# Pool weights in a buffer of their own, decay matrices from float32r products, and the last output part's products cut in two

## The chip, the cores and the metric

One core of one Trainium2 chip runs the whole program. The metric is the device time of one execution in microseconds, and a kernel's time is the median over its runs. The engines are PE (TensorE: matmul, with PEld for its weight loads), DVE (VectorE), ACT (ScalarE), POOL (GpSimd) and SP (SyncE), which here issues nearly all DMAs.

## The reference, cut to what matters

One layer of a streaming encoder runs for 1024 prompt tokens and 8 x 16 sample tokens, 1152 columns in all, D = 1024:

```
x = x + 1/2 * SwiGLU_1(RMSNorm(x))
p = RMSNorm(x) @ W_in           # q, k, v, gate: 4 heads x 128; a, b per head; u: 4 pool groups x 128
  A: gated delta rule per head  # gc = cumsum(g); decay_ij = exp(gc_i - gc_j); chunks solved, then state passed on
     o = RMSNorm(o) * SiLU(gate)
  B: d = mean of the last 2/4/8/16 tokens - token;  z = (d @ w_pool[group]) * scale
x = x + concat(o, z) @ W_out
x = x + 1/2 * SwiGLU_2(RMSNorm(x));  y = RMSNorm(x)
```

The change is in the middle part, the mixer. It touches the decay matrix, the pool group's map `d @ w_pool`, and the product with `W_out`.

## The kernel before, in words

The columns are cut into three chunks: chunk 0 has 512, chunks 1 and 2 have 320 each. The program runs the first half step, then the mixer, then the second half step. Most products are float32r in three terms (`mm3`: hi·hi, hi·lo, lo·hi); the operands are split into hi and lo by an ACT cast and a DVE subtraction. Products inside the delta rule are plain float32; each of them stands in the trace as two MATMULs.

**The mixer's order.** The mixer runs in two blocks: A is chunk 0, B is chunks 1 and 2. Its work is cut into tasks with names such as Bm3: block, kind, index. The kinds that matter here are p, v, g (projections), m (projection of a pool group and its means), n (`mapped`: the means times `w_pool`), x (hi/lo split of the mapped means), w and t (`prework` of a head, prompt and sample), y and z (inverses), c and s (the chain of states), and o (split of the gated head output, then `out_part`: 96 matmuls of 320 columns in block B). A loop written out by hand (`rule`, `fill`, `urgent`) picks the next piece of a task by a clock `T.t`, which adds a price for each product (columns / 2400 + 0.003 us for float32r, max(columns, weight columns) / 600 us for float32) and a latency that each `yield` names. A task in `fill` runs when no `urgent` one is due. A scheduler below that settles the order on each engine, so one changed price can move many instructions.

**What the change touches**, by the names and lines of this kernel:

- `means` (L1379): at its end, L1412 and L1413, it takes the small slot `wpl` in region A6 and asks for the group's 128 x 128 pool weights. `wpl` is one slot. It also holds the sample history `so` of block B (L1392), which is copied out by a DMA to `spool` (L1394), so the pool weights can't land before that DMA has read it.
- `mapped` (L1416): per chunk one float32 product `wpl` x `z` into a ps_d bank, then an ACT scale.
- `prework` (L1098): L1119 makes the decay differences, one 128 x 128 float32 product for each 128 tokens: the column of `gfl` spread over 128 as weights, a triangular matrix as the moving operand. There are 16 of them in block A and 20 in block B, 36 in all.
- `out_part` (L1071) and `oz_split` (L1084): task o splits the gated output of its head (`ozh`, `ozl`, 640 columns at once), then multiplies it and the mapped means (`om`) with the same output weights, for 2 halves of the weights, 2 chunks and 4 row tiles. The head's products and the means' products of one row tile stand together in one ps_d bank.
- Task x of index 3 waits for task o of index 2, since both use the one `omh`, `oml` pair in region B3.

The PSUM tags a, b, c and d have two banks each; the chain uses c, the inverses and prework b, the projections a, the output products and `mapped` d. The second half step opens with products for chunk 0 (`ps_b<-A,O`, `ps_a<-A,O`, 512 columns), which don't need the mixer's last results.

Of the kernel before, what the change touches and what calls it, by code (L numbers as in the profile page):

```python
# [40 lines left out]
def trunk(ctx: ExitStack, tc: tile.TileContext, xin, s0, convst, poolst, cm_in, vec_in, small_in,  # L41
# [54 lines left out]
    def region(tag, dt=F32):  # L96
        return main.tile([P, SIZE[tag]], dt, tag=tag, name=nm(tag))
# [92 lines left out]
    def load_mix(src, kind):  # L190
        with tc.high_priority(offset=300):
            return load_unit(src)
# [713 lines left out]
    def cmat(c):  # L906
        return cm[:, c:c + P]

    ms.place(region("A5"), ("Xs", 768, 1), ("DT", 512, 1), ("MV", 512, 1), ("DTs", P, 1), ("Vns", P, 1))
    ms.place(region("A6"), ("z", WIDE, 1), ("Vc", 64, 1), ("Uc", 64, 1), ("tu", 64, 1), ("wpl", P, 1), ("sso", 4, 3), ("tt", 4, 3),  # L910
             ("half", 8, 1), ("small", 8, 1), ("nega", NH, 1), ("cout", 36, 1), ("Xss", 192, 1), ("Vc", 64, 1), ("vn", P, 2),
             ("sc", 120, 2), ("av", 80, 1), ("gm", 32, 1))
    ms.place(region("R2"), ("eglS", 32, 1), ("osbs", P, 1), ("scout", 288, 1), ("Vcs", 16, 2), ("Ucs", 16, 1), ("tus", 16, 1), ("sqr", 320, 1))
    ms.place(region("B0"), ("k", 640, 1), ("q", 640, 1), ("gate", 640, 2))
    ms.place(region("B6"), ("k", 640, 1), ("q", 640, 1), ("kd", 512, 2), ("r", P, 1), ("rs", P, 1))
    ms.place(region("B1"), ("Vn", 512, 2), ("Tt", 512, 1), ("merge", 512, 1), ("U", 512, 1))
# [35 lines left out]
    def mix_block(blk, hb, extra, zrow):  # L952
# [16 lines left out]
        def decays():  # L969

            ab = mt("raw", 640)[:16]
            for (o, n), (hi, lo) in zip(offs, H):
                pa = pt("a")[:16, :n]
                for k in range(KT):
                    T.matmul(pa, wab[:, k, :], hi[k], start=(k == 0), stop=False)
                    T.matmul(pa, wab[:, k, :], lo[k], start=False, stop=(k == KT - 1))
                V.tensor_mul(ab[:, o:o + n], pa, RS[:16, o:o + n])
            pab = pt("b")[:, :nu * 16].rearrange("p (u c) -> p u c", c=16)
            for u in range(nu):
                T.transpose(pab[:, u, :], ab[:, u * P:(u + 1) * P], ident[:16, :16])  # L980
            av = mt("av", 5, 16)[:, :nu]
            V.tensor_copy(av, pab)
            def col(i, w=4):
                return sc[:, i, :nu * 4].rearrange("p (u h) -> p u h", h=4)

            def bc(t):
                return t.unsqueeze(1).to_broadcast([P, nu, NH])

            a_, b_ = col(0), col(1)
            V.tensor_add(a_, av[:, :, 0:4], av[:, :, 8:12])  # L990
            V.tensor_add(b_, av[:, :, 4:8], av[:, :, 12:16])
            V.tensor_tensor(a_, a_, bc(small[:, 0:NH]), ALU.add)
            e_ = col(2)
            V.scalar_tensor_tensor(e_, a_, -1.0, a_, ALU.mult, ALU.min)
            A.activation(e_, e_, AF.Exp)
            A.activation(e_, e_, AF.Ln, bias=1.0)
            V.scalar_tensor_tensor(a_, a_, 0.0, e_, ALU.max, ALU.add)
            V.tensor_tensor(a_, a_, bc(nega), ALU.mult)
            A.activation(b_, b_, AF.Exp, scale=-1.0)
            V.tensor_scalar(b_, b_, 1.0, None, ALU.add)  # L1000
            V.reciprocal(b_, b_)
            yield 7
            pc = pt("b")
            T.matmul(pc[:, 0:16], cmat(C_TRI), gfl[:, 0:16], start=True, stop=True)
            T.matmul(pc[:, 20:36], cmat(C_STRIL), gfl[:, 0:16], start=True, stop=True)
            T.matmul(pc[:, 40:56], ones, gfl[:, 0:16], start=True, stop=True)
            if nu == 5:
                T.matmul(pc[:, 16:20], cmat(C_TRIS), gfl[:, 16:20], start=True, stop=True)
                T.matmul(pc[:, 36:40], cmat(C_STRILS), gfl[:, 16:20], start=True, stop=True)
                gm = mt("gm", NB, NH)  # L1010
                V.tensor_tensor(gm, cm[:, C_IND:C_IND + 8].unsqueeze(2).to_broadcast([P, NB, NH]),
                                gfl[:, 16:20].unsqueeze(1).to_broadcast([P, NB, NH]), ALU.mult)
                T.matmul(pc[:, 64:96], ones, gm.rearrange("p b h -> p (b h)"), start=True, stop=True)
            V.tensor_copy(gc, pc[:, 0:nu * 4])
            A.activation(negegc, gc, AF.Exp)
            V.tensor_scalar(negegc, negegc, -1.0, None, ALU.mult)
            A.activation(ekd, pc[:, 20:20 + nu * 4], AF.Exp)
            A.activation(egl[:, :16], pc[:, 40:56], AF.Exp)
            if nu == 5:
                A.activation(eglS.rearrange("p b h -> p (b h)"), pc[:, 64:96], AF.Exp)  # L1020
            yield 4
# [46 lines left out]
            A.activation(y[:, :nt], y[:, :nt], AF.Silu)  # L1068
            return y

        def out_part(h, *parts):  # L1071
            for j in range(2):
                w = load_mix(wout[2 * h + j], 'o')
                for (o, n), c in zip(offs, chunks):
                    for d in range(4):
                        po = pt("d")[:, :n]
                        for i, (hi, lo) in enumerate(parts):
                            mm3(po, w[0][:, 4 * i + d, :], w[1][:, 4 * i + d, :], hi[:, o:o + n], lo[:, o:o + n], i == 0, i == 1)
                        x = xk(c, 4 * j + d)
                        with tc.high_priority(offset=0):  # L1080
                            V.tensor_add(x, x, po)  # L1081
                        yield 0

        def oz_split(src, hi=None, lo=None, e=None):  # L1084
            if hi is None:
                hi, lo = mt("ozh", 640), mt("ozl", 640)
            A.copy(hi[:, :nt], src)  # L1087
            (e or V).tensor_sub(lo[:, :nt], src, hi[:, :nt].bitcast(F32))
            return hi, lo

        def p3(n):
# [6 lines left out]
        def prework(h, q, k, v, samp):  # L1098

            c0, n, u0 = (512, 1, 4) if samp else (0, 4, 0)  # L1100
            tri = cmat(C_TRIS if samp else C_TRI)
            low = cmat(C_LOWS if samp else C_LOW)
            kc = [k[:, c0 + u * P:c0 + (u + 1) * P] for u in range(n)]
            qc = [q[:, c0 + u * P:c0 + (u + 1) * P] for u in range(n)]
# [11 lines left out]
            pg = p3(n)  # L1116
            for u in range(n):
                i = (u0 + u) * 4 + h
                T.matmul(pg[:, u], gfl[:, i:i + 1].to_broadcast([P, P]), tri, start=True, stop=True)  # L1119
            DT = get("DT", n, P)  # L1120
            for u in range(n):
                i = (u0 + u) * 4 + h
# [255 lines left out]

        def means(g):  # L1379
            win_ = WINS[g]  # L1380
            w = load_mix(win[16 + g], 'm')
            raw = mt("raw", WIDE)
            sv = raw[:, 527:527 + NB * 31].rearrange("p (b t) -> p b t", b=NB)
# [15 lines left out]
            for src, base, dst, L in parts:  # L1399
# [9 lines left out]
                    rec = cm[:, C_REC + g * 16:C_REC + g * 16 + 16]  # L1409
                    V.tensor_tensor(sm[:, 0, 0:16], sm[:, 0, 0:16], rec, ALU.mult)  # L1410
                V.scalar_tensor_tensor(dst, sm, 1.0 / win_, src[:, :, HIST:], ALU.mult, ALU.subtract)
            wpl = mt("wpl", P)  # L1412
            SY.dma_start(wpl, wpool_in[g])  # L1413
            return z, wpl

        def mapped(g, z, wpl):  # L1416
# [2 lines left out]
                T.matmul(ps, wpl, z[:, o:o + n], start=True, stop=True)  # L1419
                A.mul(z[:, o:o + n], ps, vec[:, 80 + g:81 + g])  # L1420

        kq, gt, pv, pw, pws, mz, om = {}, {}, {}, {}, {}, {}, {}

        def part_of(w, h):

# [31 lines left out]
                mapped(NH - 1 - h, *mz[h])  # L1457
                yield 0.8
            if w == "x":
                om[h] = oz_split(mz[h][0][:, :nt], mt("omh", 640), mt("oml", 640))  # L1460
                yield 1.5
            if w == "o":
                oz = oz_split(gt[h][:, :nt])
                yield 1.5
                yield from out_part(h, oz, om[h])
                return 0.5
            if w == "r":
                for c in (1, 2):
                    for _ in rstd_parts(c, pair(z2, mt("sqr", 320)), R[c], step=1):
                        yield 2  # L1470
# [47 lines left out]
            return spill()  # L1518
        return blocks[b](w, int(name[2]))

    names = [b + w + str(h) for b in "AB" for w in "pvgmowycnx" for h in range(NH)] + ["Ad0", "Bd0", "Ar0", "BH0", "BX0"]
    names += ["B" + w + str(h) for w in "tzs" for h in range(NH)]
    after = {n: set() for n in names}

# [6 lines left out]
        return n[:2] + str(i) if i >= 0 else "A" + n[1] + str(i + NH) if n[0] == "B" and "A" + n[1] + "0" in after else None  # L1531

    for n in names:
        if n[1] in "dHXr":
            continue
        b, w, h = n[0], n[1], n[2]
        need = {"w": "pvd", "y": "w", "t": "pvd", "z": "t", "c": "yg", "s": "zg", "n": "m", "x": "n", "o": "cx"}.get(w, "")
        rule(n, *[b + i + ("0" if i == "d" else h) for i in need])
        behind = {"v": "wt", "c": "c", "m": "n" if b == "A" else "nx", "x": "xo"}.get(w, w)
        for i in behind:  # L1540
            rule(n, prev(b + i + h))
        if w in "wt":
            rule(n, prev(b + ("c" if w == "w" else "s") + h, 2))
        if w == "m" and b == "A":
            rule(n, prev("Ax" + h, 2))
        if w == "o" and b == "B":
            rule(n, "Bs" + h)
        if w in "pgvmd" and b == "B":
            rule(n, "BH0")
        if b == "B" and w in "ts" or n in ("Bp2", "Bg2"):  # L1550
            rule(n, "BX0")
    rule("Ap3", "Ac0")
    rule("Ag3", "Ao0")
    rule("Bp0", "Ac1")
# [10 lines left out]
    for n in after:  # L1565
        after[n] &= set(names)

    fill = "Av0 Ap0 Av1 Ag0 Am0 Ap1 Ap2 Ag1 Av2 Ag2 Ao0 Am1 Ap3 Av3 Am2 Am3 Ao1 Ag3 Ao2 Bp0 Bg0 Bv0 Ao3 Bp1 Bv1 Bm0 Bg1 Bp2 Bv2 Bm1 Bp3 Bo0 Bg2 Bv3 Bo1 Bm2 Bg3 Bm3 Bo2 Bo3".split()
    urgent = [n for n in names if n not in fill]
    rank = {w: i for i, w in enumerate("drHXcsywtxnz")}  # L1570
    urgent.sort(key=lambda n: (n[0], rank[n[1]], n[2]))
# [221 lines left out]
```

## Time and profile before

| what | us |
|---|---|
| median of 3 runs (2152.22 to 2154.87) | 2153.16 |
| the profiled execution's own time | 2155.54 |
| its span | 2153.7 |
| PE busy in it | 2102.3 |
| the mixer's stretch, roughly | 740 to 1358 of the span |

Times inside the profile are microseconds from the start of the span. A busy PE is a PE with a matmul in flight; the start of a matmul is given, its end is modelled, so the time of one in a dense run is read from start to start. An entry in square brackets behind a timeline row is the idle time of the engine before it and who ended it.

### The profile page before, as it was taken

To read this page: it belongs to the slowest core of one execution; us is meant where nothing else is said; L and a number is where in the kernel's file an instruction comes from. 1 tells how busy PE (TensorE), PEld (TensorE's weight loads), DVE (VectorE), ACT (ScalarE), POOL (GpSimd) and SP (SyncE) were. 2 spreads that over 40 slices of the span, in tenths; PEclk is the share of its full clock that TensorE was granted. 3 is DMA by queue.
4 is the path that set the end of the run, shared out by engine and by line. 5 is a ranking of instruction groups with operands and counts; after the bars stand their busy time and mean duration, and the time that the engine had idled before them with its cause. 6 is when DMAs were issued, how large, how long until landed. Compare 5 with 4: busy or idle time off the path is not lost. (4 is left out here: it accounts for less than half of the span.)

```text
span 2153.7 us, 34922 instructions
## 1 busy us (share of the span) xinstructions
PE 2102.3 (98%) x13219; PEld 1942.2 (90%) x13219; DVE 1496.8 (69%) x2926; ACT 953.5 (44%) x1960; POOL 500.0 (23%) x471
## 2 busy tenths in 40 slices
PE   8999999999999999999999998999999999999997
PEld 6889999999789997887999997888999999978997
DVE  7987555567537887878687876877755556754777
ACT  6444344344313445645555445544444444432333
POOL 1344333332001200100111100134433333200121
PEclk9999999999999999999999999999999999999999
DMA  7334333358365732122222222442433334836572
GB/s 256 125 111 134 109 118 114 132 182 280 108 243 171 274 100 70 50 66 65 69 83 81 64 86 91 166 134 98 130 109 118 111 135 176 287 108 244 187 276 79
DMA packets 104407, 298.21 MB, mean 138 GB/s; under 512 B 16432, under 2 KB 24496, under 8 KB 103472
## 3 DMA queue, kind: packets, MB, share of 16 engines
q1 hardware_dynamic: 102944, 294.63, 40.2%
q8 instruction: 104, 1.70, 0.3%
q10 hardware_dynamic: 1296, 1.36, 0.2%
q14 instruction: 63, 0.52, 0.1%
HBM read 223.28 MB, written 72.66 MB: 137 GB/s over the span
## 5 line engine op out<-in xcount | busy, mean ns | idle before, releaser
L59 PE MATMUL ps_a<-B,O 128*128 128x320 f32 x3040 | 507.1, 311 | 12.5 <-DVE x L473 7.3
L59 PEld LDWEIGHTS ps_a<-B,O 128*128 128x128 f32 x3040 | 458.8, 189 | 18.0 <-DVE x L473 9.3
L59 PE MATMUL ps_a<-A,O 128*128 128x320 f32 (+1 forms) x2048 | 446.7, 354 | 1.7 <-DVE x L712 1.5
L59 PEld LDWEIGHTS ps_a<-A,O 128*128 128x128 f32 x2048 | 346.3, 188 | 38.9 <-ACT O L288 2.0
L59 PE MATMUL ps_d<-A,O 128*128 128x512 f32 (+1 forms) x1632 | 320.9, 353 | 6.0 <-ACT O L186 4.8
L59 PEld LDWEIGHTS ps_d<-A,O 128*128 128x128 f32 x1632 | 270.5, 189 | 52.9 <-ACT O L186 8.0
L289 DVE TENSOR_TENSOR O<-Q,O 128x512 fp32r<-128x512 f32 (+1 forms) x238 | 185.9, 785 | 119.6 <-ACT O L288 118.6
L288 ACT CAST O<-Q 128x512 fp32r<-128x512 f32 (+1 forms) x238 | 143.1, 605 | 175.4 <-PE ps_b L59 44.8
L59 PE MATMUL ps_b<-A,O 128*128 128x256 f32 (+2 forms) x1128 | 207.1, 334 | 5.7 <-ACT O L288 5.7
L289 DVE TENSOR_TENSOR O<-R,O 128x512 fp32r<-128x512 f32 (+1 forms) x204 | 155.6, 768 | 66.6 <-ACT O L288 66.1
L59 PE MATMUL ps_b<-B,O 128*128 128x320 f32 x1248 | 200.9, 309 | 0.0
L59 PEld LDWEIGHTS ps_b<-A,O 128*128 128x128 f32 x1128 | 175.4, 191 | 25.9 <-ACT O L288 5.9
L59 PEld LDWEIGHTS ps_b<-B,O 128*128 128x128 f32 x1248 | 186.4, 188 | 0.0
L288 ACT CAST O<-R 128x512 fp32r<-128x512 f32 (+1 forms) x204 | 123.9, 612 | 120.8 <-PE ps_d L59 35.5
L186 ACT CAST O<-R 128x1024 fp32r<-128x1024 f32 (+1 forms) x86 | 85.8, 1008 | 176.5 <-PE ps_d L59 128.0
L59 PE MATMUL ps_c<-B,O 128*128 128x320 f32 x912 | 144.9, 309 | 0.6 <-DVE O L289 0.6
L59 PEld LDWEIGHTS ps_c<-B,O 128*128 128x128 f32 x912 | 136.0, 188 | 1.3 <-DVE O L289 0.9
L187 DVE TENSOR_TENSOR O<-R,O 128x1024 fp32r<-128x1024 f32 (+1 forms) x86 | 101.7, 1189 | 50.2 <-ACT O L186 30.9
L419 POOL TENSOR_TENSOR A<-A,A 128x512 fp32r<-128x512 f32 x44 | 70.0, 1592 | 240.0 <-ACT A L418 239.9
L59 PE MATMUL ps_d<-B,O 128*128 128x320 f32 (+1 forms) x576 | 117.4, 347 | 1.8 <-ACT B L1087 1.0
L59 PEld LDWEIGHTS ps_d<-B,O 128*128 128x128 f32 x576 | 92.1, 189 | 11.0 <-DVE x L1081 2.0
L389 ACT CAST x<-x 128x320 fp32r<-128x320 f32 x98 | 44.8, 458 | 98.5 <-DMA g_keep<-x 33.2
(332 smaller groups left out, 3013.1 us busy)
## 6 DMA issues: line engine op xcount, KB each, us to landing
g_keep<-x SPq DMA_DIRECT2D x98, 320.0 KB, 3.1
R<-in_wu SPq DMA_DIRECT2D x51, 512.0 KB, 3.7
R<-in_wg SPq DMA_DIRECT2D x50, 512.0 KB, 3.8
R<-in_wd SPq DMA_DIRECT2D x48, 512.0 KB, 3.8
g_keep<-A SPq DMA_DIRECT2D x44, 512.0 KB, 3.7
A<-g_keep SPq DMA_DIRECT2D x44, 512.0 KB, 6.2
B<-g_keep SPq DMA_DIRECT2D x56, 320.0 KB, 6.9
A<-g_keep SPq DMA_DIRECT2D x42, 320.0 KB, 4.7
```

The costliest lines, as they stand in the source:

```text
L59: self.put(nc.tensor.matmul(out, lhs, rhs, **k), n / 2400 + .003 if lhs.dtype == F32R else max(n, lhs.shape[-1]) / 600)
L186: A.copy(hi, raw)
L187: (e or V).tensor_sub(lo, raw, hi.bitcast(F32))
L288: Blocks.high = A.copy(hi, src).ins
L289: Blocks.mark = V.tensor_sub(lo, src, hi.bitcast(F32)).ins
L389: A.copy(go[:, 0], src)
L419: G.tensor_sub(go[:, 1], row, go[:, 0].bitcast(F32))
```

## The change

Five edits, all in the mixer:

1. The pool weights get a slot `wp` of their own in region R2, and `means` asks for them at its start, at a priority 300 places ahead.
2. The triangular matrices are copied once into a float32r tile `exact`, `gfl` is split once per block into hi and lo (`gfls`), and each float32 decay product becomes two float32r products of the same shape, hi and lo, into the same bank.
3. `oz_split` casts and subtracts chunk by chunk.
4. A new task Bq3 (`out_ahead`) runs ahead of Bo3: it loads the first half of the last output weights and issues the means' products of six of the eight row tiles into banks a, d, a, d, b, b. Bo3 then adds the head's products to these banks.
5. So that the mapped means of index 3 can be split before Bo2 has ended, they go to region B4 instead of the shared pair, and Bx3 no longer waits for Bo2.

```diff
+    exact = const.tile([P, 2 * P], F32R, tag="exact", name="exact")
+    below = [exact[:, i * P:(i + 1) * P] for i in range(2)]
+    for t, c in zip(below, (C_TRI, C_TRIS)):
+        A.copy(t, cmat(c))
+    gfls = const.tile([P, 2, 20], F32R, tag="gfls", name="gfls")
-    ms.place(region("R2"), ("eglS", 32, 1), ..., ("sqr", 320, 1))
+    ms.place(region("R2"), ("eglS", 32, 1), ..., ("sqr", 320, 1), ("wp", P, 1))
...
+            V.tensor_copy(gfls[:, 0, :nu * 4], gfl)
+            V.tensor_sub(gfls[:, 1, :nu * 4], gfl, gfls[:, 0, :nu * 4].bitcast(F32))
...
+        def out_ahead(h, hi, lo):
+            w, ps = load_mix(wout[2 * h], 'o'), {}
+            for i, tag in enumerate("adadbb"):
+                (o, n), d = offs[i // 4], i % 4
+                ps[o, d] = po = pt(tag)[:, :n]
+                mm3(po, w[0][:, 4 + d, :], w[1][:, 4 + d, :], hi[:, o:o + n], lo[:, o:o + n], True, False)
+                yield 0
+            return w, ps
...
-        def out_part(h, *parts):
+        def out_part(h, *parts, ahead=None):
             for j in range(2):
-                w = load_mix(wout[2 * h + j], 'o')
+                w = ahead[0] if ahead and j == 0 else load_mix(wout[2 * h + j], 'o')
...
-                        po = pt("d")[:, :n]
+                        begun = ahead and j == 0 and (o, d) in ahead[1]
+                        po = ahead[1][o, d] if begun else pt("d")[:, :n]
                         for i, (hi, lo) in enumerate(parts):
+                            if begun:
+                                if i == 0:
+                                    mm3(po, w[0][:, d, :], w[1][:, d, :], hi[:, o:o + n], lo[:, o:o + n], False, True)
+                                continue
...
-            A.copy(hi[:, :nt], src)
-            (e or V).tensor_sub(lo[:, :nt], src, hi[:, :nt].bitcast(F32))
+            for o, n in offs:
+                A.copy(hi[:, o:o + n], src[:, o:o + n])
+                (e or V).tensor_sub(lo[:, o:o + n], src[:, o:o + n], hi[:, o:o + n].bitcast(F32))
...
-                T.matmul(pg[:, u], gfl[:, i:i + 1].to_broadcast([P, P]), tri, start=True, stop=True)
+                for s in range(2):
+                    T.matmul(pg[:, u], gfls[:, s, i:i + 1].to_broadcast([P, P]), below[samp], start=s == 0, stop=s == 1)
...
         def means(g):
+            wpl = mt("wp", P)
+            with tc.high_priority(offset=300):
+                SY.dma_start(wpl, wpool_in[g])
...
-            wpl = mt("wpl", P)
-            SY.dma_start(wpl, wpool_in[g])
...
-                om[h] = oz_split(mz[h][0][:, :nt], mt("omh", 640), mt("oml", 640))
+                if blk == 1 and h == NH - 1:
+                    t = region("B4", F32R)
+                    to = t[:, :640], t[:, 640:1280]
+                else:
+                    to = mt("omh", 640), mt("oml", 640)
+                om[h] = oz_split(mz[h][0][:, :nt], *to)
...
+            if w == "q":
+                begun[h] = yield from out_ahead(h, *om[h])
...
-            rule(n, prev(b + i + h))
+            if n != "Bx3" or i != "o":
+                rule(n, prev(b + i + h))
+    rule("Bq3", "Bx3", "Bo2")
+    rule("Bo3", "Bq3")
```

`fill` ends in "Bo2 Bq3 Bo3" instead of "Bo2 Bo3".

**Order on SP, around the last pool weights.** A_696 is region A6 with the old slot, R_697 is region R2 with the new one; in_wpool are the pool weights, out_spool the sample history, in_wg and in_wu weights of the second half step. Before:

```order
L1394 DMA out_spool<-A_696_7502 128x120
L1413 DMA A_696_7502<-in_wpool 128x128
L369 DMA Q_13104<-in_wg 128x1024
L1612 DMA out_ppool<-A_653_7052 128x60
L1394 DMA out_spool<-A_696_7502 128x120
L369 DMA R_1398_13108<-in_wg 128x1024
L370 DMA R_1395_13105<-in_wu 128x1024
L1413 DMA A_696_7502<-in_wpool 128x128
L1359 DMA out_sdelta<-x_1024_10072 128x1024
```

Now:

```order
L178 DMA R_1375_13058<-in_wout 128x1024
L1408 DMA R_697_7507<-in_wpool 128x128
L369 DMA Q_13165<-in_wg 128x1024
L1649 DMA out_ppool<-A_653_7052 128x60
L1422 DMA out_spool<-A_696_7506 128x120
L369 DMA R_1399_13169<-in_wg 128x1024
L370 DMA R_1396_13166<-in_wu 128x1024
L1384 DMA out_sdelta<-x_1024_10100 128x1024
```

The last pool weights stood behind the last out_spool and two half-step weights; now they stand ahead of all of these.

**Order on PE, the first head's decay products in block A** (Q is the triangular matrix, A_696 holds `gfl`). Before:

```order
L63 MATMUL ps_b_7683<-ident,B_698_7504 128x128 x4
L59 MATMUL ps_b_7692<-Q_7499,A_696_7502 128x128 x4
L59 MATMUL ps_a_7755<-A_658_7057,O_727_7750 128x512
L59 MATMUL ps_a_7755<-A_656_7055,O_728_7751 128x512
L59 MATMUL ps_a_7755<-A_656_7055,O_727_7750 128x512
```

Now:

```order
L63 MATMUL ps_b_7689<-ident,B_698_7508 128x128 x4
L59 MATMUL ps_b_7698<-exact,gfls 128x128 x8
L59 MATMUL ps_a_7765<-A_658_7057,O_727_7760 128x512
L59 MATMUL ps_a_7765<-A_656_7055,O_728_7761 128x512
L59 MATMUL ps_b_7721<-B_698_7508 128x128 x4
```

Four float32 products (two MATMULs each in the trace) became eight float32r ones; the next group of the head moved up by a few rows.

**Order on PE, the end of the mixer** (B_702 is region B3 with `ozh` and `ozl`, B_703 the raw head output that is transposed, B_1340 the mapped means in region B4, ps_b of 512 columns the second half step). Before:

```order
L59 MATMUL ps_d_12909<-B_702_7508,O_1348_12828 128x320 x2
L59 MATMUL ps_d_12909<-B_702_7508,O_1349_12829 128x320
L63 MATMUL ps_c_12917<-ident,B_703_7509 128x128 x2
L59 MATMUL ps_b_13140<-A_1387_13072,O_1404_13142 128x512
L59 MATMUL ps_b_13140<-A_1389_13074,O_1404_13142 128x512
L59 MATMUL ps_d_12933<-B_702_7508,O_1364_12929 128x320
L59 MATMUL ps_d_12941<-B_702_7508,O_1364_12929 128x320
L59 MATMUL ps_b_13140<-A_1387_13072,O_1404_13142 128x512 x2
```

Now:

```order
L63 MATMUL ps_c_12970<-ident,B_703_7513 128x128 x4
L59 MATMUL ps_d_12976<-B_702_7512,O_1351_12895 128x320 x2
L59 MATMUL ps_d_12976<-B_702_7512,O_1352_12896 128x320
L59 MATMUL ps_d_12976<-B_702_7512,O_1351_12895 128x320 x2
L59 MATMUL ps_d_12976<-B_702_7512,O_1352_12896 128x320
L59 MATMUL ps_d_12994<-B_1340_12839,O_1365_12986 128x320 x2
L59 MATMUL ps_d_12994<-B_1340_12839,O_1366_12987 128x320
L59 MATMUL ps_a_12998<-B_1340_12839,O_1366_12987 128x320
L59 MATMUL ps_b_13006<-B_1340_12839,O_1365_12986 128x320 x2
L59 MATMUL ps_d_13002<-B_1340_12839,O_1365_12986 128x320 x2
L59 MATMUL ps_d_13002<-B_1340_12839,O_1366_12987 128x320
L59 MATMUL ps_b_13006<-B_1340_12839,O_1366_12987 128x320
```

Behind the head's last transposes stood products that need the head's own split at once; now six matmuls of Bo2 and thirteen of the means stand there, and the first product that needs the split (`ps_a_12990<-B_702`) comes after those 19. Ahead of the transposes, behind the chain's last product, there were 13 matmuls of Bo2 up to the first two transposes; there are 30 now, up to all four.

## Rows read from the trace of the kernel before

**Rows 1.** The page's busy time of each engine, and the busy time by stage (columns: stretch, its length, then PE, PEld, DVE, ACT and POOL busy with the number of instructions, PE's granted clock, DMA share, GB/s): the mixer, its end, the dense opening of the second half step, and the place behind it.
```profile
PE 2102.3 (98%) x13219; PEld 1942.2 (90%) x13219; DVE 1496.8 (69%) x2926; ACT 953.5 (44%) x1960; POOL 500.0 (23%) x471
740.00:1310.00 570.00, 565.81 (x3590) 503.98 (x3589) 457.44 (x1231) 299.13 (x730) 59.80 (x130) 1.00 0.23 74
1310.00:1345.00 35.00, 28.64 (x177) 25.60 (x177) 24.02 (x54) 13.44 (x33) 2.88 (x3) 0.95 0.36 114
1345.00:1480.00 135.00, 134.54 (x667) 115.53 (x666) 104.78 (x156) 64.01 (x103) 35.48 (x21) 1.00 0.41 140
1480.00:1510.00 30.00, 25.91 (x170) 24.65 (x169) 28.73 (x38) 14.62 (x28) 14.24 (x9) 1.00 0.31 104
```

**Rows 2.** Who PE waited for between 730 and 1345 us, longest in total first (columns: total us, times, longest).
```profile
PE ps_d L59 <- DMA A<-in_wpool: 2.7, 1, 2.7
PE ps_c L63 <- ACT B L1267: 1.9, 2, 1.3
PE ps_d L59 <- ACT B L1087: 1.0, 1, 1.0
```

**Rows 3.** PE's timeline around the last pool map (start, us, what), and the two ten-microsecond stretches there with PE's granted clock (the third number from the right).
```profile
1315.42 0.38 PE L59 MATMUL ps_c<-B,B 128*128 128x128 f32 x2
1318.48 1.07 PE L59 MATMUL ps_d<-A 128*128 128x320 f32 x2 [2.67 <-DMA A<-in_wpool]
...
1310.00:1320.00 10.00, 6.66 (x42) 5.80 (x42) 6.21 (x16) 0.42 (x1) 1.47 (x2) 0.94 0.72 223
1320.00:1330.00 10.00, 10.00 (x66) 9.52 (x66) 6.07 (x14) 5.93 (x16) 0.00 (x0) 0.89 0.33 108
```

**Rows 4.** The DMA queue of SP before that map, the previous group's map on PE, and how long the eight loads of pool weights took from issue to landing.
```profile
1295.14 0.70 PE L59 MATMUL ps_d<-A 128*128 128x320 f32 x2
1311.50 0.34 SPq L1394 DMA_DIRECT2D out_spool<-A  x1
1313.08 0.33 SPq L1413 DMA_DIRECT2D A<-in_wpool  x1
DMA to landing us min/median/max: 1.7/1.9/5.3
```

**Rows 5.** PE, ACT and DVE at the end of the last chain (timelines of the three engines).
```profile
1333.72 0.39 PE L59 MATMUL ps_c<-A,B 128*128 128x128 f32 x2
1333.86 2.15 PE L59 MATMUL ps_d<-B,O 128*128 128x320 f32 x13
1337.36 0.62 PE L63 MATMUL ps_c<-ident,B 128*128 128x128 f32 x2 [1.34 <-ACT B L1267]
1337.73 2.01 PE L59 MATMUL ps_d<-B,O 128*128 128x320 f32 x12
1339.58 0.38 PE L63 MATMUL ps_c<-ident,B 128*128 128x128 f32 x2
1340.30 0.73 PE L59 MATMUL ps_b<-A,O 128*128 128x512 f32 x2 [0.34 <-ACT O L288]
1342.08 0.56 PE L59 MATMUL ps_d<-B,O 128*128 128x320 f32 x2 [1.04 <-ACT B L1087]
1336.90 1.28 ACT L1267 ACTIVATE B<-B,A 128x128 f32<-128x128 f32 x4 [1.49 <-POOL A L1265]
1340.18 0.74 DVE L1273 SCALAR_TENSOR_TENSOR B<-B,vec,ps_c 128x512 f32<-128x512 f32 x1
```

**Rows 6.** What one matmul takes, from start to start: float32 decay products (128 columns), float32 products of 32 columns, and dense float32r runs of 320 and of 256 columns.
```profile
816.88 1.06 PE L59 MATMUL ps_b<-Q,A 128*128 128x128 f32 x8
817.69 1.63 PE L59 MATMUL ps_a<-A,O 128*128 128x512 f32 x6
...
1291.76 0.97 PE L59 MATMUL ps_c<-R,x 128*128 128x32 f32 x8
1292.57 1.26 PE L59 MATMUL ps_a<-A,O 128*128 128x320 f32 x7
...
1700.39 1.93 PE L59 MATMUL ps_b<-B,O 128*128 128x320 f32 x12
1702.15 1.60 PE L59 MATMUL ps_b<-A,O 128*128 128x256 f32 x12
1703.59 1.93 PE L59 MATMUL ps_c<-B,O 128*128 128x320 f32 x12
```

**Rows 7.** Short operations of the kind that the change adds (groups by line; columns: busy us, mean ns, idle before): hi/lo splits of 320 columns, and one small DVE operation.
```profile
L389 ACT CAST x<-x 128x320 fp32r<-128x320 f32 x98 | 44.8, 458 | 98.5 <-DMA g_keep<-x 33.2
L390 DVE TENSOR_TENSOR x<-x,x 128x320 fp32r<-128x320 f32 x42 | 21.1, 501 | 12.9 <-ACT x L389 12.9
L1087 ACT CAST B<-A 128x640 fp32r<-128x640 f32 x4 | 2.9, 725 | 0.1
L1088 DVE TENSOR_TENSOR B<-A,B 128x640 fp32r<-128x640 f32 x4 | 3.3, 824 | 0.6 <-ACT B L1087 0.6
798.25 0.17 DVE L991 TENSOR_TENSOR A<-A 128x16 f32<-128x16 f32 x1
```

**Rows 8.** The load of the table with the triangular matrices (issue on SP, and landing of the program's two loads of that tensor), and the ACT row before which the copies into `exact` now stand.
```profile
737.88 0.43 SPq L904 DMA_DIRECT2D Q<-in_cm  x1
DMA to landing us min/median/max: 5.6/6.7/7.7
745.40 0.62 ACT L288 CAST O<-O 128x512 fp32r<-128x512 f32 x1 [0.98 <-PE ps_a L59]
```

More of the change, by code (lines that the diff above doesn't have):

```diff
@@ L912, in trunk @@
              ("sc", 120, 2), ("av", 80, 1), ("gm", 32, 1))
-    ms.place(region("R2"), ("eglS", 32, 1), ("osbs", P, 1), ("scout", 288, 1), ("Vcs", 16, 2), ("Ucs", 16, 1), ("tus", 16, 1), ("sqr", 320, 1))
+    ms.place(region("R2"), ("eglS", 32, 1), ("osbs", P, 1), ("scout", 288, 1), ("Vcs", 16, 2), ("Ucs", 16, 1), ("tus", 16, 1), ("sqr", 320, 1), ("wp", P, 1))
     ms.place(region("B0"), ("k", 640, 1), ("q", 640, 1), ("gate", 640, 2))
@@ L1100, in prework @@
             c0, n, u0 = (512, 1, 4) if samp else (0, 4, 0)
-            tri = cmat(C_TRIS if samp else C_TRI)
             low = cmat(C_LOWS if samp else C_LOW)
@@ L1420, in mapped @@
                 A.mul(z[:, o:o + n], ps, vec[:, 80 + g:81 + g])
-        kq, gt, pv, pw, pws, mz, om = {}, {}, {}, {}, {}, {}, {}
+        kq, gt, pv, pw, pws, mz, om, begun = {}, {}, {}, {}, {}, {}, {}, {}
         def part_of(w, h):
@@ L1464, in part_of @@
                 yield 1.5
-                yield from out_part(h, oz, om[h])
+                yield from out_part(h, oz, om[h], ahead=begun.get(h))
                 return 0.5
+            if w == "q":
+                begun[h] = yield from out_ahead(h, *om[h])
             if w == "r":
@@ L1519, in task @@
         return blocks[b](w, int(name[2]))
-    names = [b + w + str(h) for b in "AB" for w in "pvgmowycnx" for h in range(NH)] + ["Ad0", "Bd0", "Ar0", "BH0", "BX0"]
+    names = [b + w + str(h) for b in "AB" for w in "pvgmowycnx" for h in range(NH)] + ["Ad0", "Bd0", "Ar0", "BH0", "BX0", "Bq3"]
     names += ["B" + w + str(h) for w in "tzs" for h in range(NH)]
@@ L1533, in trunk @@
     for n in names:
-        if n[1] in "dHXr":
+        if n[1] in "dHXrq":
             continue
@@ L1566, in trunk @@
         after[n] &= set(names)
-    fill = "Av0 Ap0 Av1 Ag0 Am0 Ap1 Ap2 Ag1 Av2 Ag2 Ao0 Am1 Ap3 Av3 Am2 Am3 Ao1 Ag3 Ao2 Bp0 Bg0 Bv0 Ao3 Bp1 Bv1 Bm0 Bg1 Bp2 Bv2 Bm1 Bp3 Bo0 Bg2 Bv3 Bo1 Bm2 Bg3 Bm3 Bo2 Bo3".split()
+    fill = "Av0 Ap0 Av1 Ag0 Am0 Ap1 Ap2 Ag1 Av2 Ag2 Ao0 Am1 Ap3 Av3 Am2 Am3 Ao1 Ag3 Ao2 Bp0 Bg0 Bv0 Ao3 Bp1 Bv1 Bm0 Bg1 Bp2 Bv2 Bm1 Bp3 Bo0 Bg2 Bv3 Bo1 Bm2 Bg3 Bm3 Bo2 Bq3 Bo3".split()
     urgent = [n for n in names if n not in fill]
```

## The prediction

> **What bounds the kernel now.** I read the busy times first: PE has a matmul in flight for 2102.3 us of the 2153.7 us span, DVE for 69% of it [rows 1]. So a microsecond is gained only where PE works less or waits less. By stage, PE waits 4.2 us in the 570 us of the mixer's body, but 6.4 us in the 35 us of its end, where its granted clock is also down to 0.95; the 135 us that follow are dense again, and the next gap is at 1480, 4.1 us in 30, where DVE is busy 28.7 of 30 [rows 1]. The list of PE's waits then names the end: 2.7 us for the pool weights, 1.9 us for the ACT scaling of the head's output, 1.0 us for the split of that output [rows 2]. PE's timeline shows where each stands [rows 3, 5], SP's queue shows why the weights were late [rows 4], and the start times of dense runs give the price of one matmul [rows 6].
>
> **The change part by part.** The sum is made against the profiled execution, 2155.54 us (span 2153.7); that run is 2.4 us above the median of 2153.16, and I take the gain off the median.
>
> 1. *The last pool weights.* They are asked for at 1313.08, only after the sample history's DMA at 1311.50, and they land 5.3 us later, against a median of 1.9, while the half step's weights move too [rows 4]; PE's map of that group waits 2.67 us [rows 3], and the chain's products stand behind it in PE's queue. In the new order the load stands ahead of out_spool. It still has to wait for PE, since one slot serves all groups, but for the map of the group before, which ended by about 1296 [rows 4]. With 5.3 us to land it is there by 1301, some 14 us early. The 2.67 us go. A load that waits on SP holds up what is behind it: here a half-step weight that isn't needed for another 40 us. The first load now stands in the first half step's last part, where SP waits for PE a few instructions later anyway. I put both at nothing; if that cover were gone, it is one landing, 5.3 us.
>
> 2. *The clock behind that wait.* PE's granted clock is 0.94 of full speed in 1310 to 1320 and 0.89 in 1320 to 1330 [rows 3], that is the lower level, 1.2 GHz, for 12% and 22% of them, after the pause and at no other place in the mixer. That is 0.6 and 1.1 us of full-speed work lost. Part of the first may lie in the pause, so it is between 1.1 and 1.7; I take 1.4.
>
> 3. *The end of the chain.* Before, 13 matmuls cover the time from the chain's last product to the first transposes, and PE waits 1.34 us, then 0.34, then 1.04 [rows 5]: 2.72 us. From 1333.72 to 1337.36 the transposes are ready after 3.64 us. Now 30 matmuls of 0.147 us (1.76 us for 12 [rows 6]) stand there, 4.4 us. So PE doesn't wait, and the transposes come some 0.8 us later than they could, but all four together. From the last transposes to the first product of the head's split it took 2.5 us (1339.58 to 1342.08), of it 0.74 on DVE and a cast of 0.725 [rows 5, 7]. The cast is now 320 columns, 0.458 [rows 7], so 2.2 us. The 19 matmuls behind the transposes cover 2.8 us. All 2.72 us go. The products themselves are only moved: PE does the 18 of the means earlier, and half-step products that filled these gaps later.
>
> 4. *The decay products.* 36 float32 products are 72 MATMULs, and they become 72 of float32r. The old ones start 0.101 us apart (0.81 us for 8). Float32 products of 32 columns start just as far apart, 0.81 us for 8 [rows 6], so the columns don't set it. Float32r with 128 columns isn't in this trace. From below: 320 columns take 0.147 us and 256 take 0.120 [rows 6], 0.42 ns a column, which would give 0.067 at 128. From above: no more than 256 columns, 0.120. So between 2.4 us gained and 1.4 lost. The nearest row in shape is the 32-column one, since every MATMUL loads 128 columns of weights; I take 0.100, a gain of 0.1 us.
> The Trainium skill, page "TensorE: Matmul & The Clock Gate", section "LDWEIGHTS (loading the stationary operand)", says that loading weights takes their columns divided by 1.2 GHz, which is 107 ns for 128; by it this part would be a loss of 0.4 us, and the rows at 0.101 agree nearly.
>
> 5. *What is added.* Two ACT copies into `exact`, each under 0.458 us [rows 7], now stand before a cast that started at 745.40 after 0.98 us of idling; the table, asked for at 737.88, lands between 743.5 and 745.6 [rows 8]. They delay that cast by 0 to 1.1 us; I take 0.2. Eight splits in block B become sixteen: 2 x 0.458 for 0.725 on ACT and 2 x 0.501 for 0.824 on DVE [rows 7], 1.5 us on either engine. DVE has 113 us to spare in the mixer's body, ACT 271 [rows 1], so nothing; without that cover 1.5. Four DVE operations of 0.17 us for `gfls` [rows 7] lie in the same cover.
>
> 6. *The new order.* The lower price of the decay products in the planner's clock moves several hundred rows on PE and more on DVE. The waits of the mixer's body were 4.2 us [rows 1]; they can vanish or double. In the last chain two products now stand behind shorter fillers. I take a loss of 0.4.
>
> Sum: 2.67 + 1.4 + 2.72 + 0.1 - 0.2 - 0.4 = 6.3 us, 2149.2 for the profiled execution and **2146.9** for the median. Is it given back later? The next gap, at 1480, is DVE working on operands in PE's own pace; DVE had slack before it (105 of 135 us busy [rows 1]), so it moves forward with the rest.
>
> **The rivals.**
>
> - *Float32r at 128 columns runs by its columns.* At 0.067 us the gain is 2.4 instead of 0.1: 2144.6. For it: the straight line through 256 and 320 columns. Against it: the 32-column row. Chance 0.15. The same page, section "Back-to-back issue gap", gives 56 ns for 128 columns when weights cost nothing; by that it would be 3.2 us gained, and no row here is that short.
> - *Short float32r costs as many passes as float32.* If one of the new MATMULs does all the passes that a pair did, it takes 0.202 us, and 72 x 0.101 = 7.3 us are lost: 2153.16 - 6.2 + 7.3 = 2154.3, slower than before. It decides from 0.19 us a MATMUL upwards. For it: no float32r product under 256 columns stands in this trace. Against it: 256 columns take 0.120 in the dense runs. Chance 0.07.
> - *The end finds a new wait.* The six started tiles hold both banks of a, b and d until the head's split is there, so the half step's opening products can't fill PE any more. If the split is late by 2.7 us, the gain of part 3 is gone: 2149.6. Against it: 2.8 us of cover for 2.2. Chance 0.11.
> - *The new order waits more.* If the body's waits double, 4.2 us are lost instead of 0.4: 2150.7. Chance 0.09.
> - *The weights come no earlier.* If SP reaches the last load late, behind the wait for the map or for the history, parts 1 and 2 stay: 2151.0. Against it: their place in the queue. Chance 0.04.
>
> **How the numbers follow.** My forecast has 0.54. About 0.2%, 4.3 us, is what a measurement can tell from no change, so the line is at 2148.9. Faster: the forecast nearly whole (0.51) and the first rival, 0.66. Within: three rivals, the rest of the forecast and most of the second, 0.30. Slower needs the second rival with a worse order, 0.04. The range goes down to 2143.0, the first rival with the clock's upper bound and no loss in the order, and up to 2151.8, over the last two rivals; it leaves out the second rival and the ends of the others.
>
> **What would show it.** In the new profile: no wait of PE for in_wpool and a clock of 1.00 around the last map (parts 1, 2); the last in_wpool issue near 1296 and long before its use; after the last transposes no PE idle time for ACT's split, and the ps_a, ps_d, ps_b products of the means there (part 3); a run of `ps_b<-exact,gfls` x8 taking about 0.8 us from start to start, 0.53 for the first rival and 1.6 for the second (part 4); PE's waits in the mixer's body still near 4 us (part 6); the gap behind the half step's opening unchanged in length. I am wrong if PE's idle time at the mixer's end is still above 3 us, or if the decay products are far from 0.1 us each.

## The result

The changed kernel is slower: 2161.39 us (2157.63 to 2164.81, 13 runs) beside 2153.16 of before, ratio 1.0037 with a 95% interval of 1.0027 to 1.0046, that is 5.8 to 9.9 us lost. Its profiled execution took 2159.07 us, 2.3 below its median, while that of the kernel before took 2155.54, 2.4 above its own: the two traces lie 3.5 us apart, the medians 8.2.

The profile after, page and stages as in [rows 1] (stretch, length, busy time of PE, PEld, DVE, ACT, POOL, PE's granted clock, DMA share, GB/s):

```profile
PE 2104.2 (98%) x13219; PEld 1941.3 (90%) x13219; DVE 1496.9 (69%) x2938; ACT 953.3 (44%) x1970; POOL 498.8 (23%) x471
740.00:1310.00 570.00, 559.59 (x3525) 495.84 (x3523) 451.47 (x1226) 292.29 (x720) 59.96 (x128) 1.00 0.23 73
1310.00:1345.00 35.00, 31.81 (x221) 28.96 (x220) 24.70 (x60) 16.21 (x45) 3.53 (x4) 1.00 0.38 125
1345.00:1480.00 135.00, 134.41 (x659) 114.43 (x658) 106.60 (x163) 67.59 (x112) 31.86 (x19) 1.00 0.40 137
1480.00:1510.00 30.00, 25.93 (x172) 24.94 (x171) 26.75 (x34) 13.29 (x26) 14.87 (x10) 1.00 0.28 92
```

The end of the mixer is denser, as forecast, and its clock is whole. The loss is in the first row of the mixer: PE is idle for 10.4 of 570 us, where it was 4.2. Who PE waited for, in the stretch of [rows 2]:

```profile
PE ps_d L59 <- DVE x L1105: 2.5, 5, 0.8
PE ps_b L59 <- ACT B L1156: 2.4, 3, 0.9
PE ps_b L63 <- ACT B L1156: 1.8, 2, 1.0
PE ps_c L59 <- DVE B L1326: 1.7, 1, 1.7
PE ps_c L59 <- DVE B L1313: 1.4, 1, 1.4
```

No pool weights any more. L1156 is ACT's scaling of a head's transposed keys, in `prework`: five waits, 4.2 us, each shortly behind a group of decay products. Before, that line (L1131 there) held PE up for 0.18 us once. The first line, PE waiting for DVE's additions into x, is 2.2 us more in the mixer's body than before (0.3 there); with the 4.0 of L1156 that is the 6.2 us. PE's and ACT's timelines at the first head:

```profile
818.15 1.09 PE L59 MATMUL ps_b<-exact,gfls 128*128 128x128 f32 x8
819.08 0.68 PE L59 MATMUL ps_a<-A,O 128*128 128x512 f32 x2
820.66 1.16 PE L59 MATMUL ps_b<-B 128*128 128x128 f32 x8 [0.90 <-ACT B L1156]
...
819.45 1.16 ACT L1156 ACTIVATE B<-ps_b,A 128x128 f32<-128x128 f32 x4
```

The keys' products (third row) need the bank that ACT still reads. Before, six products of 512 columns filled this time [rows 6]; now two do. Four of them are some 0.9 us, which is the wait. The eight decay products take 0.93 us, start to start, where [rows 6] had 0.81.

At the place of [rows 3, 4], the map, the clock and SP's issue of the last pool weights:

```profile
1328.48 0.70 PE L59 MATMUL ps_d<-A,R 128*128 128x320 f32 x2
...
1310.00:1320.00 10.00, 10.00 (x76) 9.17 (x75) 5.10 (x14) 6.60 (x20) 0.54 (x1) 1.00 0.19 54
1320.00:1330.00 10.00, 8.49 (x53) 6.96 (x52) 8.58 (x22) 2.43 (x6) 1.96 (x2) 1.00 0.47 151
...
1302.55 0.33 SPq L1408 DMA_DIRECT2D R<-in_wpool  x1
```

And the end of the last chain, as in [rows 5]:

```profile
1337.15 0.49 PE L59 MATMUL ps_c<-B,B 128*128 128x128 f32 x2 [1.68 <-DVE B L1326]
...
1341.80 4.68 PE L59 MATMUL ps_d<-B,O 128*128 128x320 f32 x30
1346.31 0.60 PE L63 MATMUL ps_c<-ident,B 128*128 128x128 f32 x4
1347.23 1.81 PE L59 MATMUL ps_d<-B,O 128*128 128x320 f32 x9 [0.31 <-DVE x L1105]
1348.88 0.31 PE L59 MATMUL ps_a<-B,O 128*128 128x320 f32 x1
1349.02 0.45 PE L59 MATMUL ps_b<-B,O 128*128 128x320 f32 x2
```

The transposes come in one go and no wait for the head's split follows; but two products of the chain now wait, 1.40 and 1.68 us. What held up the second, on ACT and on DVE (each with its idle time before it; DVE's L1326 is what PE waited for):

```profile
1334.94 2.58 ACT L250 ACTIVATE A<-x,vec 128x512 fp32r<-128x512 f32 x4 [3.22 <-DMA x<-x_keep]
...
1335.69 0.75 DVE L251 SCALAR_TENSOR_TENSOR A<-x,vec,A 128x512 fp32r<-128x512 f32 x1 [2.14 <-ACT A L250]
1336.36 0.48 DVE L1105 TENSOR_TENSOR x<-x,ps_d 128x320 f32<-128x320 f32 x1
1336.76 0.34 DVE L1326 SCALAR_TENSOR_TENSOR B<-B,A,ps_c 128x128 f32<-128x128 f32 x1
```

ACT waits for columns of x that are loaded again for the second half step (L250), DVE waits for ACT (L251), and the chain's own step L1326 stands behind that in DVE's queue. The experiments e6 to e9 come back to this load.

### The profile page after: what moved, and what is told of

The parts are those of the page before. It is cut to its first block, busy times and chain, and to the rows that moved or that the text cites. A ratio compares the mean times of both kernels' runs of the same rounds, so it can differ in the third digit from the quotient of the medians.

```text
span 2157.3 us, 34947 instructions
## 1 busy us (share of the span) xinstructions
PE 2104.2 (98%) x13219; PEld 1941.3 (90%) x13219; DVE 1496.9 (69%) x2938; ACT 953.3 (44%) x1970; POOL 498.8 (23%) x471
## 3 DMA queue, kind: packets, MB, share of 16 engines
q10 hardware_dynamic: 1296, 1.36, 0.2%
```

## The experiments

Each was timed in five rounds; the ratio is to the kernel before on the same chip, whose median there was 2152.8 to 2153.2. "Idle" is PE's idle time in 740 to 1310 and in 1310 to 1375 of the profiled execution, worked out from the stage rows.

| run | what it is | median, us | ratio (95%) | idle, us |
|---|---|---|---|---|
| before | | 2153.16 | | 4.2, 6.8 |
| after | all five edits | 2161.39 | 1.0037 (1.0027 to 1.0046) | 10.4, 3.8 |
| e1 | without edit 2 | 2151.44 | 0.9986 (0.9978 to 0.9995) | 3.9, 4.9 |
| e2 | all, old price in the planner | 2160.34 | 1.0035 (1.0022 to 1.0049) | 11.1, 5.1 |
| e3 | before, with the low price alone | 2154.12 | 1.0000 (0.9992 to 1.0009) | 4.2, 4.3 |
| e4 | edit 2 alone | 2160.20 | 1.0032 (1.0022 to 1.0042) | 11.5, 3.8 |
| e5 | all, decay products 256 wide | 2151.60 | 0.9998 (0.9990 to 1.0007) | 5.2, 4.9 |
| e6 | edit 1 alone | 2150.24 | 0.9987 (0.9978 to 0.9995) | 4.0, 3.5 |
| e7 | edits 3, 4, 5 alone | 2150.64 | 0.9992 (0.9984 to 1.0001) | 4.2, 3.9 |
| e8 | e6, with four scalings deferred | 2149.20 | 0.9988 (0.9978 to 0.9999) | 4.0, 5.3 |
| e9 | e1, with four scalings deferred | 2146.65 | 0.9971 (0.9962 to 0.9980) | 4.0, 2.2 |

**e1: edit 2 undone.** The lines with `exact`, `below` and `gfls` go, and

```diff
-                for s in range(2):
-                    T.matmul(pg[:, u], gfls[:, s, i:i + 1].to_broadcast([P, P]), below[samp], start=s == 0, stop=s == 1)
+                T.matmul(pg[:, u], gfl[:, i:i + 1].to_broadcast([P, P]), tri, start=True, stop=True)
```

> The changed kernel with float32 decay products again (edit 2 undone, edits 1, 3, 4, 5 kept), so with the planner's old price for them too. Theory O (the lower price reorders the mixer's body, PE's idle time in 740 to 1310 went from 4.2 to 10.4 us): the idle time is near 4 again and edits 1, 3, 4, 5 bring what they were to bring (2.7 + 1.4 + 2.7), 2146 to 2149. Theory P (float32r of 128 columns takes 0.116 us instead of 0.101 and that is all that edit 2 costs, 1.1 us): 2160. Theory E (the products ahead and the early load cost more at the mixer's end than they bring): 2158 to 2161.

Edit 2 is the loss: without it the body's idle time is 3.9 us. But the other edits bring 1.1 to 4.7 us, not 6.8, and the time lies above what theory O asked.

**e2: the planner's price kept.**

```diff
-                     n / 2400 + .003 if lhs.dtype == F32R else max(n, lhs.shape[-1]) / 600)
+                     max(n / 2400 + .003, lhs.shape[-1] / 1200) if lhs.dtype == F32R else max(n, lhs.shape[-1]) / 600)
```

> The changed kernel with all five edits, but the planner's clock charges a pair of float32r decay products what it charged the float32 product, 0.213 us. Theory O: idle time of the body near 4, 2147 to 2150, that is the first experiment plus 1.1 us for the 72 products. Theory P: as the changed kernel, 2160 to 2162. Theory E: the same, 2160 to 2162.

A miss for theory O as I had put it: with the old price the five waits for L1156 are there (4.5 us in the mixer's body; columns as in [rows 2]). The low price in the planner's clock isn't the cause.

```profile
PE ps_b L59 <- ACT B L1156: 2.8, 3, 1.1
PE ps_b L63 <- ACT B L1156: 1.7, 2, 0.8
```

**e3: the planner's price alone.**

```diff
                 T.matmul(pg[:, u], gfl[:, i:i + 1].to_broadcast([P, P]), tri, start=True, stop=True)
+                T.t -= P / 600 - 2 * (P / 2400 + .003)
```

> The kernel before, whose planner's clock charges each float32 decay product 0.113 us instead of 0.213; no instruction is added or removed, only the order differs. Theory O: PE's idle time in the mixer's body rises to about 10 us, 2158 to 2161. Theories P and E: 2152 to 2154, as before.

The other half of that miss: this order differs from the one before on PE too, and no loss is clear of the noise (the interval is 1.7 us gained to 1.9 lost), with the body's idle time at 4.2 us. It does bring a 1.28 us wait of the chain, like the 1.40 us one of the changed kernel.

**e4: edit 2 alone**, the lines of e1 the other way round, in the kernel before.

> The kernel before with edit 2 alone (float32r decay products and the low price that comes with them). Theory O: new waits of some 6 us and 1.1 us for the products, 2159 to 2163. Theory P: 2154 to 2155. Theory E: 2153 to 2155.

The whole loss is there, 2.2 to 4.2 thousandths, with no other edit. So it comes with the float32r products, but not through the planner, and their 0.116 us apiece accounts for 72 x 0.116 - 72 x 0.101 = 1.1 us of it only. What is left is the scheduler below the planner, or the products themselves.

**e5: the same products, 256 columns wide.** The order on PE, which is settled before the program runs, shows what the scheduler does: one float32 product per 128 tokens leaves six products of 512 columns behind the first head's group, two float32r products of 128 columns leave two; two of 256 columns leave six.

```diff
+    exact = const.tile([P, 6 * P], F32R, tag="exact", name="exact")
...
+            for a in range(0, n, 2):
+                some = range(a, min(a + 2, n))
+                for s in range(2):
+                    for u in some:
+                        i, c = (u0 + u) * 4 + h, (3 * samp + 1 - (u - a)) * P
+                        T.matmul(bank[:, a * P:(a + 2) * P], gfls[:, s, i:i + 1].to_broadcast([P, P]), exact[:, c:c + 2 * P],
+                                 start=s == 0 and u == a, stop=s == 1 and u == some[-1])
```

> The changed kernel, all five edits, with the same 72 float32r decay products made 256 columns wide: the triangular matrix stands between blocks of zeros, two neighbouring 128-column results form one accumulation, and the second 128 columns of a product add zeros. The order on PE becomes that of the kernel before again (6 instead of 2 products of 512 columns behind the first head's decay products). Theory S (the scheduler under the planner charges a float32r product of 128 columns as much as a whole float32 product, 0.21 us, so it believes each head's pair to be 0.85 us longer than it is and leaves that much less other work ahead of the next product, which then waits for ACT): PE's idle time in 740 to 1310 is near 4 again instead of 10.4, the waits for ACT's scaling of the head's keys (4.2 us in six places) are gone, and the time is that of the first experiment plus 72 x 0.120 - 36 x 0.202 = 1.4 us: 2152 to 2154. Theory F (float32r decay products make PE wait on the chip whatever the order): idle time 9 to 12, 2160 to 2163.

The order and the waits are as theory S has them. PE's timeline at the same place:

```profile
818.18 1.17 PE L59 MATMUL ps_b<-exact,gfls 128*128 128x256 f32 x8
819.18 1.56 PE L59 MATMUL ps_a<-A,O 128*128 128x512 f32 x6
820.69 1.16 PE L59 MATMUL ps_b<-B 128*128 128x128 f32 x8
```

The products are longer (0.125 us) and twice as wide, no wait for this scaling over 0.15 us is left at any head, the waits for the additions into x are gone from the body too, its idle time is 5.2 us, and the ratio falls by 0.0039. (The waits stood in five places, not six; the median is 0.4 us below the forecast.) The wider products also raise the planner's price of a pair, to 0.219 us, but e2 charged 0.213 and kept the waits; between e2 and e5 the width is what changed, and with it the order. So the order is shown to be the cause of the waits. Why the scheduler chose it is not shown: what it charges isn't written in the kernel, and that it is about 0.2 us for a 128-column float32r product is inferred from the places it left empty.

**e6 and e7: the rest of the sum, in two halves.** e6 has edit 1's lines alone, e7 those of edits 3, 4 and 5.

> The kernel before with edit 1 alone: the pool weights' own slot and early request. If parts 1 and 2 of the sum hold as they stand, 2.7 + 1.4 us less than before: 2148 to 2150. If the gap at the second half step's opening (4.1 us in 1480 to 1510 before, 5.5 behind the earlier end in the first experiment) or new waits at the mixer's end take it back: 2151 to 2153.

> The kernel before with edits 3, 4 and 5 alone: split by chunks, the means' products of the last output part ahead, no early pool weights. If part 3 of the sum holds, 2.7 us less than before: 2149 to 2151. If the two waits that the first experiment showed at this place (2.0 us for the addition into x behind ps_d, 1.6 us for the head's split) stand here too, they take the gain: 2152 to 2155.

Each median gains less than its term, 2.8 us of 4.1 (interval 1.1 to 4.7) and 1.7 of 2.7 (-0.2 to 3.4), but neither interval excludes the term. In e7 PE's idle time at the end fell by 2.9 us, as forecast; with both halves together, in e1, it fell by only 1.9. Nothing is given back at the half step's opening: its five gaps add up to 6.2 us before and to 5.9 and 5.7 here. The missing part is at the mixer's end. In e6 (ACT, DVE and PE, each with the idle time before it):

```profile
1323.09 0.72 ACT L250 ACTIVATE A<-x,vec 128x512 fp32r<-128x512 f32 x1 [4.32 <-DMA x<-x_keep]
...
1323.85 0.75 DVE L251 SCALAR_TENSOR_TENSOR A<-x,vec,A 128x512 fp32r<-128x512 f32 x1 [2.68 <-ACT A L250]
1324.52 0.48 DVE L1081 TENSOR_TENSOR x<-x,ps_d 128x320 f32<-128x320 f32 x1
...
1325.05 0.41 PE L59 MATMUL ps_d<-B,O 128*128 128x320 f32 x1 [2.01 <-DVE x L1081]
```

L250 and L251 scale and split columns of x for the second half step; their load (`x<-x_keep`) was issued at 1319.38. ACT stands for it, DVE's L251 for ACT, and behind L251 in DVE's queue is the addition that frees PE's ps_d bank. Before, this load went out at the same time (1319.64), but ACT, behind the chain that the pool weights had held up, came to it only at 1325.31 and didn't wait. e1 has the same 1.98 us, and 1.55 more for the head's split.

**e8 and e9: that load covered again.** Its four later scalings on ACT are issued behind one of the chain's last copies:

```diff
...
-            A.copy(osb, po)
+            late.append(A.copy(osb, po).ins)
...
-            scale_split(0, wi, *H)
+            scale_split(0, wi, *H, range(4))
+            with tc.issue_after(late[-3]):
+                scale_split(0, wi, *H, range(4, KT))
```

> Edit 1 alone, as in the sixth experiment, and ACT's four scalings of the half step's reloaded columns (those that waited for the load of x_keep until 1323.09, with the chain's work behind them on ACT and the additions into x behind them on DVE) are issued behind the chain's second last but one copy, some 4 us later. Theory Q (the early pool weights uncovered this load: in-order ACT and DVE carried its lateness to PE, 2.0 us): the 2.0 us wait for the addition into x is gone, and the time is 1.5 to 2 us below the sixth experiment, 2148 to 2149. Theory R (the additions are late for another reason, or the half step then starts late): the wait stays or moves, 2150 to 2152.

> The first experiment (edits 1, 3, 4 and 5, float32 decay products) with the same deferred scalings. Theory Q: the 2.0 us wait is gone, the wait of 1.6 us for the head's split stays (11 matmuls lie behind the transposes instead of 19), 2148.5 to 2150. Theory R: 2151 to 2153. If both this and the eighth hold, the one with the lower median is the version to keep.

In e8 the wait fell to 0.95 us, but the time didn't follow: the median is 1.0 lower than in e6, the ratio to the kernel before the same (0.9988 and 0.9987). The waits at the very end of the chain, which edit 1 doesn't touch and which are absent in e6, are back as in [rows 5] (1.33, 0.34, 1.04), and the end's idle time rose from 3.5 to 5.3 us. So e8 is a miss for the time that theory Q asked. e9, which differs from e1 by the deferral alone, is clearer: 6.2 us less than before (4.3 to 8.2), idle time at the end 2.2 us against e1's 4.9; the intervals of e1 and e9 just overlap (from 0.9978, up to 0.9980). ACT and PE there, and the stage:

```profile
1321.19 2.58 ACT L250 ACTIVATE A<-x,vec 128x512 fp32r<-128x512 f32 x4 [0.76 <-DMA x<-x_keep]
...
1323.15 0.56 PE L59 MATMUL ps_d<-B,O 128*128 128x320 f32 x2 [0.56 <-DVE x L1100]
...
1336.13 0.41 PE L59 MATMUL ps_a<-B,O 128*128 128x320 f32 x1
...
1310.00:1375.00 65.00, 62.83 (x375) 56.28 (x374) 57.84 (x120) 33.95 (x73) 5.11 (x5) 1.00 0.45 156
```

The first product of the head's split (third row) doesn't wait, against 1.55 us in e1 that I had expected to stay; I read this as the chain not being held up any more, which no run tests by itself. e9 beats both kernels. The deferral without the five edits was not run, so how much of the 6.2 us it would bring alone stays open.

## Why the prediction was wrong

The step that failed is part 6, the new order. It read the move of several hundred rows as the work of the planner's lower price, and bounded its cost by "they can vanish or double", with 0.4 us taken. Both were wrong. The planner's price brings no loss clear of noise by itself (e3), and the old price doesn't take the waits away (e2). The scheduler below it left some 0.9 us less other work behind the 128-column pairs of a head, and PE waited: the body's idle time went from 4.2 to 10.4 us, 6.2 lost where the sum had 0.4. That this scheduler took the pairs for about 0.9 us longer per head than the float32 products is inferred, from the order that came back with the width (e5). The order rows that stood ahead of the prediction showed it: in the second pair of listings the keys' products stand only two products behind the decay products. I wrote that they had moved up and didn't ask what then covers ACT's 1.16 us of scaling.

The rival "the new order waits more" had the right place and the wrong size, 4.2 us, and it still credited the other parts in full. The range's lower end, 2143.0, doesn't follow from the terms named for it, which give 2144.6 - 0.3 - 0.4 = 2143.9; nothing hangs on it here. By step:

1. *The pool weights*: right. No wait, issue at 1302.55, used at 1328.48 (I had said 1296; the map of the group before, which the load follows, came some 6 us later too). But "Is it given back later?" had an answer that I missed, having looked only at the gap at 1480: the reload of x, 2.01 us in e6, and 1.68 in the changed kernel itself.
2. *The clock*: 1.00 from 1310 to 1330 in the changed kernel, as forecast, but that is in part luck. In e6, without the wait for the pool weights, the same stretch was granted 0.91; in e3, with 1.71 us of that wait, 1.00. So no run shows the 1.4 us as a price of that wait; the last section shows that the clock behind one and the same pause differs between traces.
3. *The chain's end*: right that the head's split is covered there. In place of its 2.7 us two waits of the last chain stand, 3.1 us. The first, 1.40, belongs to the "shorter fillers" of part 6: e3 has it too. The second, 1.68, is the reload of x again, a wait that the sum had nowhere. So the sign that I had named, more than 3 us of idle time at the mixer's end, came true: 3.2 in 1310 to 1345. In e9 the end has 2.2 us of idle time in 65 instead of 6.8.
4. *The decay products*: mechanism right, size off: 0.116 us against 0.100 taken, inside the bounds, 1.1 us lost instead of 0.1 gained. The two rivals on their price are out. The Trainium skill, "TensorE: Matmul & The Clock Gate", section "LDWEIGHTS (loading the stationary operand)", gives 107 ns by the 128 weight columns; the rows lie at 116, nearer to it than to my value.
5. *What is added*: nothing is seen of it. The copies into `exact` took 0.49 us at 745.76, and the next cast still waited for PE.

With one more load moved out of the way, edits 1, 3, 4 and 5 bring 6.2 us (4.3 to 8.2) against the 6.6 that I forecast for them. That the two agree is in part luck, since the sum held 1.4 us for the clock and e9 also holds the deferral. Edit 2 costs some 10 us (e1 to after). In the profiles its body waits are 6.5 us of that and the products 1.1; some 2 us are spread over the run and not attributed. Of the 8.2 us between the medians of before and after, the two traces show 3.5: 6.2 more idle time in the body and 1.1 for the products, less 3.0 at the end and what the clock gave back. The other 4.7 they don't show.

## What to carry to other kernels

Where two layers set the order, look for the price that each of them charges for an instruction: a few short products can move the work that covers somebody else's latency, and their width can be enough to change it. In an order listing, count the rows between a group and the next user of its bank, and set them against the time of the engine that frees the bank. When a stall is taken away, list the loads issued in the microseconds behind it and who, in order, stands behind their first reader; a gain at one place needs the next cover too.

## What the runs showed of the hardware

- A float32r matmul of 128 columns takes 0.116 us from start to start, one of 256 columns 0.125 in the same place: the narrower one saves next to nothing. A float32 product of 128 columns, two MATMULs, takes 0.202, so a pair of float32r products, 0.232, has nothing to gain over it.
- A pause of PE is not always followed by a lower clock: behind 2.01 us in e6 the stretch 1310 to 1375 was granted 0.97, behind 1.98 us at the same place in e1 1.00. The work around the pause doesn't settle it either: near 44 us, ahead of all that the edits move, all eleven traces have the same products around the same 3.1 us of waiting for POOL, and 40 to 60 was granted 1.00 in five of them (before, e2, e3, e6, e8), 0.91 in four and 0.83 in two; in the trace of after, PE is at 0.50, the lower level of 1.2 GHz, from 47 to 53. A clock seen in one trace is no price of an edit.
